# Rests of the first weight tiles by accumulating DMA instead of GpSimd, masks made one layer earlier, and another pool of banks for the last down steps (hybrid two-layer network, 1 core)

## The chip, the core and the metric

The kernel runs on one core of one Trainium2 chip. The metric is the device time of one execution in microseconds. A core has a matrix engine (PE), a vector engine (DVE), a scalar engine (ACT), GpSimd (POOL), a sync engine (SP) that issues most loads, and 16 DMA engines that all queues share.

## The reference

256 tokens of width 2048 go through two layers. Each layer is a mixer and a conv-FFN, and after each of the four comes a residual sum and a layer norm. All is in fp32.

```python
def conv_ffn(x, w_up, conv_w, conv_b, w_down):          # D_FF = 5632, CONV_W = 3
    h = x @ w_up
    hc = conv_b + conv_w[CONV_W - 1] * h
    for j in range(CONV_W - 1):
        hc = hc + conv_w[j] * shift_right(h, CONV_W - 1 - j)
    a, v = jnp.split(hc, 2, axis=-1)
    return (jax.nn.silu(a) * v) @ w_down
...
    for l in range(DEPTH):                               # DEPTH = 2
        if l % 2 == 0:
            mix = jnp.concatenate([ya, yb], axis=-1) @ ev_w_out[e]   # gated unit, window means
        else:
            h = x @ od_w_in[o]
            q, f_logit, inp, g = jnp.split(h, 4, axis=-1)
            y = hgrn2(q, f_logit, inp, lb_all[l])        # chunked linear recurrence, chunk mask tril
            y = rms_norm(y, ...) * jax.nn.sigmoid(g)
            mix = y @ od_w_out[o]
        x = layer_norm(ALPHA * x + mix, ln1_g[l], ln1_b[l])
        x = layer_norm(ALPHA * x + conv_ffn(x, ...), ln2_g[l], ln2_b[l])
```

## The kernel before, in words

**Split products.** PE multiplies numbers of type fp32r. A matrix `w` is therefore cut into a rounded part `wh` and a rest `wl = w - wh`, the activations likewise into `xh` and `xl`, and a product is summed from three matmuls, `xh*wh`, `xh*wl` and `xl*wh`. Weights come in raw tiles of 128 x 2048 fp32 (1 MB), three slots (`BUFS`), loaded by SP's queue in the order of a plan (`Weights`). `cast` (before L162 to L185) makes `wh` on ACT (L178) and `wl` by a subtraction (L181), into a ring of three pairs. A tile holds four blocks of 128 rows by 512 columns, so that one tile with one half of the tokens is 12 matmuls of 128x512. Tokens are in two halves, t = 0 and t = 1, and a stage's first `chunk` uses each of its four weight tiles first for one half, then for the other.

**Who subtracts.** `wl` is DVE's work, except for the first two tiles of each FFN and of the second layer's mixer: their numbers stand in the set `on_pool` (L168, filled in `plan_ffn` L227 and at L244), and GpSimd makes their rests, four pieces of 128x512 each.

**Heads of stages.** A stage ends with its last product, the residual sum into `x_t` (`add_x`, DVE L542 or L574), the statistics, and for each half t four pieces q = 0 to 3 of the normalization: DVE takes off the mean and multiplies by `g` (L511), multiplies by the inverse deviation `rs` and adds `b` (L512). PE then transposes a piece into `pt` (L493, four small matmuls), ACT writes `xh` from it (L279) and DVE `xl` (L280). The next stage's first product needs piece 0 of half 0. The work of a stage's end and of the next one's beginning is interleaved, and a scheduler puts each engine's instructions in one order ahead of time; an engine runs them strictly in that order. I call these three places head 1 (start of the first FFN, 240 us), head 2 (start of the second layer's mixer, 967 us) and head 3 (start of the second FFN, 1465 us).

**Banks.** PSUM has eight banks. Four are the pool `acc` (tags `ps0` to `ps3`) for the units of the FFN, which sum into them over many products; four are the pool `aux` for all else, transposes, `ph` and the down products `pd` among it. `down` (L563 on) multiplies one block of the gated hidden values by one tile of `w_down` for both halves into two `aux` banks, and DVE adds each to `x_t` (L574). The FFN's plan does four down steps beside each of the units 1 to 9, and two beside unit 10; the two left over come after unit 10 (L820 and L821), then `last_down` takes the last block.

**The masks.** The recurrence writes its attention products with a predicate `msk`, a byte tile of four copies of a triangular matrix `tri`. It is cast by DVE at the beginning of the second layer (L838 to L840).

Of the kernel before, what the change touches and what calls it, by code (L numbers as in the profile page):

```python
# [9 lines left out]
F32 = mybir.dt.float32  # L10
F32R = mybir.dt.float32r
BF16 = mybir.dt.bfloat16
U8 = mybir.dt.uint8
AF = mybir.ActivationFunctionType
ALU = mybir.AluOpType
# [3 lines left out]
P = 128  # L19
# [10 lines left out]
          ("P1", "s", "P7", "s", "P3", "P2", "P6", "o", "P5", "o", "P4", "s", "s"))  # L30
UNIT = ("P1", "s", "P2", "s", "P3", "o", "P7", "o", "P6", "o", "P5", "o", "P4", "s", "s")
BUFS = 3
EDGE = 244


class Weights:
# [3 lines left out]
    def __init__(self, nc, raw, hl, ahead):  # L40
        self.nc, self.raw, self.hl, self.ahead = nc, raw, hl, ahead

        self.feeds, self.loads = [], ([], [])
        self.n_load = [0, 0]

        self.phase = self.open = 0
        self.n_cast = self.n_take = self.n_prep = 0
        self.ring = {}
        self.done = {}
        self.on_pool = set()  # L50

        self.extra = {}

# [108 lines left out]
    def cast(self, pieces=1, between=None):  # L162
        i = self.n_cast
        w = self.feeds[i]["r"]["tile"]
        pool, tags = (self.raw[1], self.extra[i]) if i in self.extra else (self.hl, ("wh", "wl"))
        h = pool.tile([P, 4, 512], F32R, name=f"wh{i}", tag=tags[0])
        l = pool.tile([P, 4, 512], F32R, name=f"wl{i}", tag=tags[1])
        if i in self.on_pool:  # L168
            pieces, eng = 4, self.nc.gpsimd
        else:  # L170
            eng = self.nc.vector
        n = 4 // pieces
        self.prep(i + 1)
        for k in range(0, 4, n):
            if between is not None:
                between(k)
            sl = slice(k, k + n)
            self.nc.scalar.activation(h[:, sl], w[:, sl], AF.Copy)  # L178
            if k == 0:
                self.prep(i + 2)  # L180
            eng.tensor_tensor(out=l[:, sl], in0=w[:, sl], in1=h[:, sl].bitcast(F32), op=ALU.subtract)  # L181
        self.done[i] = (h, l)
        self.n_cast += 1
        if self.feeds[i]["after"]:
            self.feeds[i]["after"]()  # L185
# [17 lines left out]
def block_kernel(ctx: ExitStack, tc: tile.TileContext, a, out):  # L203
    nc = tc.nc
    V, A, G, T = nc.vector, nc.scalar, nc.gpsimd, nc.tensor

    const = ctx.enter_context(tc.tile_pool(name="const", bufs=1))
# [8 lines left out]
    acc = ctx.enter_context(tc.tile_pool(name="acc", bufs=1, space=PSUM))  # L216
    banks = ["ps0", "ps1", "ps2", "ps3"]
    aux = ctx.enter_context(tc.tile_pool(name="aux", bufs=4, space=PSUM))

    W = Weights(nc, raw, hl, 2)  # L220
# [3 lines left out]
        W.std([a["w_ev_out"][c, g] for g in (2, 3, 0, 1)])  # L224

    def plan_ffn(l):
        W.on_pool |= {len(W.feeds) + i for i in range(2)}  # L227
        W.extra[len(W.feeds) + 3] = ("q1", "q3")
        up, down = a["w_up"][l], a["w_down"][l]
        W.phase += 1  # L230
        for p in range(11):
            if p == 0:
                W.std([up[0, g] for g in range(4)])
                W.std([up[11, g] for g in range(4)])
                continue
            now = [down[c, p - 1] for c in range(4 if p < 10 else 2)]
            W.quad([up[p, 0], up[p, 1], up[11 + p, 1], up[11 + p, 0]],
                   [up[p, 2], up[p, 3], up[11 + p, 2], up[11 + p, 3]], now)
        W.std([down[c, 9] for c in (2, 3)])
        W.extra[len(W.feeds)] = ("q1", "q3")  # L240
        W.std([down[c, 10] for c in range(4)])

    plan_ffn(0)
    W.on_pool |= {len(W.feeds) + i for i in range(2)}  # L244
    W.extra[len(W.feeds) + 3] = ("qa", "qb")
    W.phase += 1
    wi, wo = a["w_od_in"], a["w_od_out"]
# [14 lines left out]

    edge.tile([P, EDGE], F32, name="edge")
    cst = const.tile([P, 3, P], F32, name="cst")
    ident, tri, aft = (cst[:, i] for i in range(3))
    mhalf = const.tile([P, 4], F32, name="mhalf")
    G.memset(mhalf, -0.5)


    def new_T(kind, g, pool=acts):  # L270
        h = pool.tile([P, 4, S], F32R, name=f"{kind}h{g}", tag=f"{kind}h{g}")
        l = pool.tile([P, 4, S], F32R, name=f"{kind}l{g}", tag=f"{kind}l{g}")
        return h, l
# [218 lines left out]
    def transpose(dst, src):  # L492
        T.transpose(dst, src, ident)  # L493
# [80 lines left out]
            V.tensor_tensor(out=xs, in0=xs, in1=ps, op=ALU.add)  # L574
        return xs

    def down(c, Ts, scale):

        w = W.take()
        for t in range(2):  # L580
            ps = aux.tile([P, 512], F32, name="pd", tag="aux")
            product(ps, w, Ts, t)
            tick(0.5)
            add_x(t, c, ps, scale)

    def last_down(get, g_ap, b_ap, final, n_skew=4):

        gt, bt = load_gb(g_ap, b_ap)
        sts = [small.tile([P, 4, 6], F32, name=f"st{t}") for t in range(2)]
        new = [new_T("x", g) for g in range(4)] if not final else None  # L590
        def out_bank():
            b = banks.pop(0)
            banks.append(b)
            return acc.tile([P, 512], F32, name="ps", tag=b)

        def after(t, c, ps):
            V.bn_stats(sts[t][:, c], add_x(t, c, ps, False))  # L597

        def norm(t, q, mean, rs):
            qs = slice(q * 512, (q + 1) * 512)  # L600
            normalize(x_t[t][:, qs], x_t[t][:, qs], mean, rs, gt[:, qs], bt[:, qs])
            if final:
                nc.sync.dma_start(out[t * P:(t + 1) * P, qs], x_t[t][:, qs])
            else:
                transpose_split(new[q], x_t[t][:, qs], t)

        tick(9)
        Ts = get()
        for c in range(4 - n_skew):
            w = W.take()  # L610
            for t in range(2):
                ps = out_bank()
                product(ps, w, Ts, t)
                after(t, c, ps)
        skewed = range(4 - n_skew, 4)
        ws = [W.take() for _ in skewed]
        for c, w in zip(skewed, ws):
            ps = out_bank()
            product(ps, w, Ts, 0)
            after(0, c, ps)  # L620
        mean, rs = moments(sts[0])
        todo = list(range(4))
        for c, w in zip(skewed, ws):
            ps = out_bank()
            product(ps, w, Ts, 1)

            while len(todo) > 3 - c:
                norm(0, todo.pop(0), mean, rs)
            after(1, c, ps)
        mean, rs = moments(sts[1])  # L630
        for q in range(4):
            norm(1, q, mean, rs)
        return new
# [4 lines left out]
    def lower_bound():  # L638
        lp = small.tile([P, 2, 16], F32, name="lp", bufs=1)
        nc.sync.dma_start(lp, a["lbT"].rearrange("p (l h) -> p l h", l=2))  # L640
        mx = small.tile([P, 16], F32, name="mx", bufs=1)
        V.tensor_tensor(out=mx, in0=lp[:, 0], in1=lp[:, 1], op=ALU.max)
        for l in range(2):
            V.tensor_tensor(out=lp[:, l], in0=lp[:, l], in1=mx, op=ALU.subtract)
        A.activation(lp, lp, AF.Exp)
        V.tensor_tensor(out=mx, in0=lp[:, 0], in1=lp[:, 1], op=ALU.add)
        V.reciprocal(mx, mx)
        for l in range(2):
            V.tensor_tensor(out=lp[:, l], in0=lp[:, l], in1=mx, op=ALU.mult)
        V.tensor_tensor(out=lp[:, 1], in0=lp[:, 0], in1=lp[:, 1], op=ALU.add)  # L650
        V.tensor_tensor(out=lp[:, 1], in0=lp[:, 1], in1=lp[:, 0], op=ALU.subtract)

        def store():
            pl = aux.tile([16, P], F32, name="pl", tag="aux")
            transpose(pl, lp[:, 1])
            row = small.tile([16, P], F32, name="row", bufs=1)
            A.activation(row, pl, AF.Copy)
            nc.sync.dma_start(lb_d, row)

        later(1, store)  # L660
# [5 lines left out]
    with tc.tile_pool(name="work0", bufs=1) as wk:  # L666
# [73 lines left out]
        gv, bv = loads0()  # L740
        chunk(XT, 4, after_v(1))
        lower_bound()
        for t in range(2):
            nc.sync.dma_start(x_t[t], a["x"][t * P:(t + 1) * P])
        chunk(XT, 4, after_b(0))
# [11 lines left out]
    def ffn(l, XT, final):  # L757
        with ExitStack() as pools:
            wk = pools.enter_context(tc.tile_pool(name=f"workf{l}", bufs=1))
# [8 lines left out]
            GT = {}  # L768
# [48 lines left out]
            for p in range(1, 11):  # L817
                downs = [lambda c=c, p=p: down(c, GT[p - 1], p == 1) for c in range(4)]
                strassen(XT, XS, h_tile, ready(p), downs[:4 if p < 10 else 2])
            for fn in downs[2:]:  # L820
                fn()  # L821
            XT = last_down(lambda: GT[10], a["ln2_g"][l], a["ln2_b"][l], final)
            del raw[1]
        return XT
# [4 lines left out]
    with ExitStack() as pools:  # L829
        yp = pools.enter_context(tc.tile_pool(name="ymix1", bufs=1))  # L830
        raw[1] = pools.enter_context(tc.tile_pool(name="rawq", bufs=1))
        wk = pools.enter_context(tc.tile_pool(name="work1", bufs=1))
# [2 lines left out]
        A.activation(tri_r, tri, AF.Copy)  # L835
        aft_r = wk.tile([P, P], F32R, name="aft_r")
        A.activation(aft_r, aft, AF.Copy)
        msk = wk.tile([P, 4, P], U8, name="msk")  # L838
        for k in range(4):
            V.tensor_copy(msk[:, k], tri)  # L840
        att = [wk.tile([P, 4, P], F32, name=f"att{t}") for t in range(2)]
        for t in range(2):
            G.memset(att[t], 0.0)
# [269 lines left out]
```

## Time and profile before

| what | value |
|---|---|
| median of 3 runs | 2197.44 us (2197.28 to 2199.90) |
| the profiled execution's own time | 2202.97 us |
| its span in the trace | 2201.2 us |
| busy: PE / weight loads / DVE / ACT / POOL | 2157.1 / 1779.9 / 1767.4 / 1230.3 / 125.8 us |
| moved by DMA | 489.00 MB |

The page gives busy time by engine, then 40 slices of the span, the DMA queues, the chain that ended last, and the costliest groups of instructions. Queries of the trace give more: `--timeline` lists an engine's instructions in order, with the idle time ahead of one and what ended it in brackets; the view of waits sums those brackets.

### The profile page before, as it was taken

What the parts mean: (1) busy time and instruction counts of PE and PEld (TensorE: products, weight loads), DVE (VectorE), ACT (ScalarE), POOL (GpSimd) and SP (SyncE); (2) the same over time, 40 slices, a digit from 0 to 9 for tenths busy, and PEclk for the clock granted to TensorE, in tenths of its full rate; (3) what the DMA queues carried; (4) which work ended last, traced back from release to release, by engine and by line L of the source; (5) the groups of instructions that cost most, each with busy time, mean ns of one, the idle gap of its engine ahead of it and who ended that gap; (6) DMA issues with size and microseconds to landing.
All of it is one profiled execution on the core that took longest, in us unless ns stands there. A gap on an engine that the chain in (4) does not pass through costs nothing. (4 is left out here: it accounts for less than half of the span.)

```text
span 2201.2 us, 24814 instructions
## 1 busy us (share of the span) xinstructions
PE 2157.1 (98%) x9887; PEld 1779.9 (81%) x9887; DVE 1767.4 (80%) x1706; ACT 1230.3 (56%) x1150; POOL 125.8 (6%) x140
## 2 busy tenths in 40 slices
PE   9999999999999999989999999999999999999997
PEld 7888788888888888878778888778888888888886
DVE  5545888888888888897687887888888888888888
ACT  5443455555655555646575756636555655555662
POOL 1000200000000000020000000030000000000000
PEclk9999999999999999999999999999999999999999
DMA  8646476777667677537778687746777666677743
GB/s 324 268 151 234 152 243 222 236 247 239 215 217 226 219 241 248 184 128 259 222 236 252 220 256 229 232 173 204 234 243 238 218 223 213 227 241 240 242 150 141
DMA packets 71796, 489.00 MB, mean 222 GB/s; under 512 B 8465, under 2 KB 9121, under 8 KB 13953
## 3 DMA queue, kind: packets, MB, share of 16 engines
q1 hardware_dynamic: 60656, 411.56, 50.0%
q0 software_dynamic: 11024, 75.86, 17.1%
q8 instruction: 77, 1.26, 0.2%
q14 instruction: 39, 0.31, 0.0%
HBM read 443.34 MB, written 2.11 MB: 202 GB/s over the span
## 5 line engine op out<-in xcount | busy, mean ns | idle before, releaser
L181 DVE TENSOR_TENSOR wl<-w,wh 128x2048 fp32r<-128x2048 f32 (+1 forms) x471 | 1051.2, 2235 | 337.7 <-ACT wh L178 334.2
L178 ACT ACTIVATE wh<-w 128x2048 fp32r<-128x2048 f32 (+1 forms) x495 | 894.7, 1813 | 628.7 <-PE pd L566 262.2
L412 PE MATMUL ps<-wh,xh 128*128 128x512 f32 x1188 | 468.0, 394 | 0.0
L412 PE MATMUL ps<-wl,xh 128*128 128x512 f32 x1188 | 462.8, 390 | 1.1 <-DVE wl L181 1.1
L412 PE MATMUL ps<-wh,xl 128*128 128x512 f32 x1188 | 462.8, 390 | 0.0
L566 PE MATMUL pd<-wh,yh 128*128 128x512 f32 x736 | 287.2, 390 | 3.2 <-DVE x L574 3.2
L566 PE MATMUL pd<-wl,yh 128*128 128x512 f32 x736 | 286.5, 389 | 0.4 <-DVE wl L181 0.4
L566 PE MATMUL pd<-wh,yl 128*128 128x512 f32 x736 | 286.4, 390 | 0.5 <-DVE yl L280 0.4
L412 PEld LDWEIGHTS ps<-wh,xl 128*128 128x128 f32 x1188 | 223.0, 188 | 46.7
L412 PEld LDWEIGHTS ps<-wl,xh 128*128 128x128 f32 x1188 | 223.3, 188 | 46.2 <-DVE wl L181 1.9
L412 PEld LDWEIGHTS ps<-wh,xh 128*128 128x128 f32 x1188 | 223.1, 188 | 45.0 <-ACT wh L178 0.4
L412 PE MATMUL ps<-wh,sh 128*128 128x512 f32 x432 | 169.8, 393 | 0.8 <-ACT u L424 0.5
L412 PE MATMUL ps<-wl,sh 128*128 128x512 f32 x432 | 168.9, 391 | 1.1 <-DVE wl L181 1.1
L412 PE MATMUL ps<-wh,sl 128*128 128x512 f32 x432 | 168.7, 390 | 0.0
L566 PEld LDWEIGHTS pd<-wh,yh 128*128 128x128 f32 x736 | 138.2, 188 | 32.5 <-DVE x L574 4.0
L566 PEld LDWEIGHTS pd<-wh,yl 128*128 128x128 f32 x736 | 138.1, 188 | 30.3 <-DVE yl L280 1.6
L566 PEld LDWEIGHTS pd<-wl,yh 128*128 128x128 f32 x736 | 138.2, 188 | 29.3 <-DVE wl L181 0.8
L341 PE MATMUL ps<-wh,xh 128*128 128x512 f32 x384 | 151.8, 397 | 1.6 <-ACT wh L178 1.6
L341 PE MATMUL ps<-wl,xh 128*128 128x512 f32 x384 | 151.2, 394 | 0.3 <-DVE wl L181 0.3
L341 PE MATMUL ps<-wh,xl 128*128 128x512 f32 x384 | 150.8, 393 | 0.0
L789 DVE SCALAR_TENSOR_TENSOR hc<-ph,cw,hc 128x254 f32<-128x254 f32 (+1 forms) x352 | 145.8, 475 | 1.4 <-ACT hc L786 1.2
L786 ACT ACTIVATE hc<-ph,cw 128x256 f32<-128x256 f32 x176 | 89.1, 556 | 62.5 <-DVE hc L789 58.8
(223 smaller groups left out, 2216.5 us busy)
## 6 DMA issues: line engine op xcount, KB each, us to landing
w<-in_w_up SPq DMA_DIRECT2D x176, 1024.0 KB, 4.9
w<-in_w_down SPq DMA_DIRECT2D x88, 1024.0 KB, 4.9
w<-in_w_od_in SPq DMA_DIRECT2D x64, 1024.0 KB, 6.6
w<-w POOLq DMA_DIRECT2D x40, 1024.0 KB, 8.1
w<-in_w_od_in POOLq DMA_DIRECT2D x21, 1024.0 KB, 9.2
w<-in_w_ev_in SPq DMA_DIRECT2D x20, 1024.0 KB, 5.2
w<-in_w_ev_out SPq DMA_DIRECT2D x16, 1024.0 KB, 4.8
w<-in_w_od_out SPq DMA_DIRECT2D x16, 1024.0 KB, 7.2
```

Source lines behind the costliest of these rows:

```text
L178: self.nc.scalar.activation(h[:, sl], w[:, sl], AF.Copy)
L181: eng.tensor_tensor(out=l[:, sl], in0=w[:, sl], in1=h[:, sl].bitcast(F32), op=ALU.subtract)
L341: T.matmul(ps[t], s[:, k, ts], m[:, k], start=(gi == 0 and k == 0 and i == 0), stop=(gi == n - 1 and k == 3 and i == 2))
L412: T.matmul(bank_, x[:, k, ts], m[:, k], start=(id(bank_) not in started), stop=(k == 3 and i == 2), skip_group_check=True)
L566: T.matmul(ps, x[:, k, t * P:(t + 1) * P], m[:, k], start=(k == 0 and i == 0), stop=(k == 3 and i == 2))
L786: A.activation(ob, pt[:, k], AF.Identity, scale=cw[:, 2, blk:blk + 1], bias=cw[:, 3, blk:blk + 1])
L789: V.scalar_tensor_tensor(out=ob[:, s:S], in0=pt[:, k, 0:S - s], scalar=cw[:, w, blk:blk + 1], in1=ob[:, s:S], op0=ALU.mult, op1=ALU.add)
```

## The change

1. **Rests.** `on_pool` becomes `on_dma`, with the same tiles. For each half (128x1024) of such a tile ACT writes `wh`, then ACT writes `wl = -wh`, and GpSimd's queue issues a DMA that adds the raw `w` into `wl` in memory (512 KB each). GpSimd computes nothing there, and ACT has four instructions of 128x1024 a tile where it had four of 128x512. The weights of the next tiles are prepared (`prep(i + 2)`) ahead of these.
2. **Masks.** `msk` becomes a constant tile; its four casts stand in the first layer, behind `lower_bound`. `EDGE` shrinks by the same 512 bytes a partition, so that the addresses behind it stay.
3. **Banks.** The two left-over down steps of each FFN (c = 2, 3) take banks of `acc` in turn (`out_bank`), which are the unit's, instead of `aux` banks.

```diff
-EDGE = 244
+EDGE = 244 - 128
...
-        if i in self.on_pool:
-            pieces, eng = 4, self.nc.gpsimd
-        else:
-            eng = self.nc.vector
+        if i in self.on_dma:
+            self.prep(i + 2)
+            for sl in (slice(0, 2), slice(2, 4)):
+                self.nc.scalar.activation(h[:, sl], w[:, sl], AF.Copy)
+                self.nc.scalar.activation(l[:, sl], h[:, sl].bitcast(F32), AF.Copy, scale=-1.0)
+                self.nc.gpsimd.dma_start(l[:, sl].rearrange("p k n -> p (k n)"),
+                                         w[:, sl].rearrange("p k n -> p (k n)"), accum_op=ALU.add)
+            self.done[i] = (h, l)
+            self.n_cast += 1
+            return
...
-            eng.tensor_tensor(out=l[:, sl], in0=w[:, sl], in1=h[:, sl].bitcast(F32), op=ALU.subtract)
+            self.nc.vector.tensor_tensor(out=l[:, sl], in0=w[:, sl], in1=h[:, sl].bitcast(F32), op=ALU.subtract)
...
+    msk = const.tile([P, 4, P], U8, name="msk")
...
-    def down(c, Ts, scale):
+    def out_bank():
+        b = banks.pop(0)
+        banks.append(b)
+        return acc.tile([P, 512], F32, name="ps", tag=b)
+
+    def down(c, Ts, scale, own=False):
...
-            ps = aux.tile([P, 512], F32, name="pd", tag="aux")
+            ps = out_bank() if own else aux.tile([P, 512], F32, name="pd", tag="aux")
...
         lower_bound()
+        for k in range(4):
+            V.tensor_copy(msk[:, k], tri)
...
-            for fn in downs[2:]:
-                fn()
+            for c in (2, 3):
+                down(c, GT[9], False, own=True)
...
-        msk = wk.tile([P, 4, P], U8, name="msk")
-        for k in range(4):
-            V.tensor_copy(msk[:, k], tri)
```

The order of the instructions moves at the heads. ACT at head 1 before: `w_40` and `w_41` are the first FFN's first two raw tiles, `xh` the four pieces of the new activations.

```order
L178 ACTIVATE wh_1589<-w_39_1497 128x2048
L178 ACTIVATE wh_1595<-w_40_1527 128x512 x4
L279 ACTIVATE xh_1157<-pt 128x4x128
L279 ACTIVATE xh_1159<-pt 128x4x128
L178 ACTIVATE wh_1607<-w_41_1563 128x512 x4
L279 ACTIVATE xh_1161<-pt 128x4x128
L279 ACTIVATE xh_1163<-pt 128x4x128
L178 ACTIVATE wh_1794<-w_42_1593 128x2048
```

ACT at head 1 in the change (its lines are numbered 7 or 8 higher):

```order
L185 ACTIVATE wh_1594<-w_39_1502 128x2048
L172 ACTIVATE wh_1600<-w_40_1532 128x1024 x2
L173 ACTIVATE wl_1601<-wh_1600 128x1024 x2
L172 ACTIVATE wh_1610<-w_41_1568 128x1024 x2
L173 ACTIVATE wl_1611<-wh_1610 128x1024 x2
L287 ACTIVATE xh_1162<-pt 128x4x128
L287 ACTIVATE xh_1164<-pt 128x4x128
L287 ACTIVATE xh_1166<-pt 128x4x128
L287 ACTIVATE xh_1168<-pt 128x4x128
L185 ACTIVATE wh_1795<-w_42_1598 128x2048
```

All eight casts of both tiles now stand ahead of the first `xh`; before, two pieces of `xh` stood between the tiles.

PE in head 1 before, at the first transposes of half 1 (`x_202`), which stood in the fourth tile (`wh_1800`):

```order
L341 MATMUL ps<-wh_1800,xh_1163 128x512
L493 MATMUL pt<-cst,x_202 128x128 x4
L341 MATMUL ps<-wl_1801,xh_1163 128x512
L493 MATMUL pt<-cst,x_202 128x128 x4
L341 MATMUL ps<-wh_1800,xl_1164 128x512
```

PE in head 1 of the change, where the same transposes (half 1 is `x_203` now) stand in the second tile (`wh_1610`):

```order
L349 MATMUL ps<-wh_1610,xh_1164 128x512
L349 MATMUL ps<-wl_1611,xh_1164 128x512
L501 MATMUL pt<-cst,x_203 128x128 x4
L349 MATMUL ps<-wh_1610,xl_1165 128x512
L501 MATMUL pt<-cst,x_203 128x128 x4
L349 MATMUL ps<-wh_1795,xh_1166 128x512
L349 MATMUL ps<-wh_1600,xh_1162 128x512
```

The transposes of half 1 moved up by some two tiles' products, and one more product of the third tile (`wh_1795`) stands behind them before half 1 begins with the first tile.

POOL at head 2, before (`w_132`, `w_133` are the mixer's first two tiles):

```order
L501 TENSOR_TENSOR rs<-rs,mhalf 128x1
L181 TENSOR_TENSOR wl_6695<-w_132_6638,wh_6694 128x512 x4
L181 TENSOR_TENSOR wl_6707<-w_133_6686,wh_6706 128x512 x4
L843 MEMSET att_6941 128x512
L843 MEMSET att_6942 128x512
L851 DMA lb<-lb_d 128x512
L501 TENSOR_TENSOR rs<-rs,mhalf 128x1
```

POOL at head 2 in the change:

```order
L509 TENSOR_TENSOR rs<-rs,mhalf 128x1
L174 DMA wl_6696<-w_132_6639 128x1024 x2
L851 MEMSET att_6933 128x512
L174 DMA wl_6706<-w_133_6687 128x1024 x2
L509 TENSOR_TENSOR rs<-rs,mhalf 128x1
L851 MEMSET att_6934 128x512
L859 DMA lb<-lb_d 128x512
```

The eight subtractions have become four DMA issues, and `rs` of half 1 stands behind those and one memset only.

## Rows read from the trace of the kernel before

**Rows 1.** The page's first part: busy time and share by engine.

```profile
PE 2157.1 (98%) x9887; PEld 1779.9 (81%) x9887; DVE 1767.4 (80%) x1706; ACT 1230.3 (56%) x1150; POOL 125.8 (6%) x140
```

**Rows 2.** PE's waits: engine, line, releaser, us in total, times, longest.

```profile
PE pt L493 <- DVE x L512: 10.8, 8, 2.7
```

**Rows 3.** Timeline of PE, head 1: start, us, instruction, [idle before <-releaser].

```profile
243.30 0.63 PE L493 MATMUL pt<-cst,x 128*128 128x128 f32 x4 [1.10 <-DVE x L512]
...
249.60 0.63 PE L493 MATMUL pt<-cst,x 128*128 128x128 f32 x4 [2.67 <-DVE x L512]
...
251.28 0.63 PE L493 MATMUL pt<-cst,x 128*128 128x128 f32 x4 [0.83 <-DVE x L512]
...
252.44 0.39 PE L341 MATMUL ps<-wh,yl 128*128 128x512 f32 x1
```

**Rows 4.** Timeline of DVE, head 1.

```profile
239.40 1.41 DVE L511 SCALAR_TENSOR_TENSOR x<-x,mv,g 128x512 f32<-128x512 f32 x2
...
243.07 3.47 DVE L511 SCALAR_TENSOR_TENSOR x<-x,mv,g 128x512 f32<-128x512 f32 x2
```

**Rows 5.** Timeline of POOL, head 1.

```profile
241.01 12.52 POOL L181 TENSOR_TENSOR wl<-w,wh 128x512 fp32r<-128x512 f32 x8 [0.44 <-ACT wh L178]
```

**Rows 6.** Timeline of ACT: a 128x1024 instruction early on, then head 1.

```profile
11.93 1.06 ACT L279 ACTIVATE xh<-xr 128x1024 fp32r<-128x1024 f32 x1 [0.62 <-DMA xr<-in_xT]
...
240.30 2.19 ACT L178 ACTIVATE wh<-w 128x512 fp32r<-128x512 f32 x4 [8.96 <-PE ps L341]
```

**Rows 7.** The DMA issues: transfer, queue, count, KB each, median us to landing.

```profile
w<-w POOLq DMA_DIRECT2D x40, 1024.0 KB, 8.1
...
lb<-lb_d POOLq DMA_DIRECT2D x4, 256.0 KB, 3.4
```

**Rows 8.** The DMA queues over the span: packets, MB, share of 16 engines.

```profile
q0 software_dynamic: 11024, 75.86, 17.1%
```

**Rows 9.** The DMA issues between 235 and 300 us.

```profile
w<-w POOLq DMA_DIRECT2D x1, 1024.0 KB, 12.3
```

**Rows 10.** Groups of POOL's instructions: count, busy us, mean ns, idle before.

```profile
L81 POOL DMA_DIRECT2D w<-w x20 | 17.2, 859 | 720.9 <-DMA w<-in_w_up 658.7 <-issue 62.2
```

**Rows 11.** Stretches: busy us of each engine, PEclk, DMA share, GB/s.

```profile
240.00:245.00 5.00, 3.90 (x22) 2.93 (x21) 5.00 (x6) 3.27 (x6) 4.56 (x4) 1.00 0.01 2
...
975.00:980.00 5.00, 3.09 (x15) 2.42 (x14) 4.29 (x8) 1.72 (x1) 3.07 (x5) 0.91 0.55 194
980.00:985.00 5.00, 5.00 (x23) 3.96 (x22) 3.39 (x6) 1.72 (x3) 0.00 (x0) 0.75 0.17 68
...
1465.00:1470.00 5.00, 3.49 (x13) 2.89 (x14) 5.00 (x7) 2.08 (x4) 5.00 (x4) 0.72 0.00 0
```

**Rows 12.** Timeline of PE, head 2.

```profile
967.68 0.66 PE L493 MATMUL pt<-cst,x 128*128 128x128 f32 x4 [0.99 <-DVE x L512]
...
972.32 0.66 PE L493 MATMUL pt<-cst,x 128*128 128x128 f32 x4 [1.24 <-DVE x L512]
...
979.02 1.03 PE L493 MATMUL pt<-cst,x 128*128 128x128 f32 x4 [1.91 <-DVE x L512]
```

**Rows 13.** Timeline of DVE, head 2.

```profile
974.93 2.08 DVE L840 CAST msk<-cst 128x128 uint8<-128x128 f32 x1
```

**Rows 14.** Timeline of PE, head 3.

```profile
1465.40 0.66 PE L493 MATMUL pt<-cst,x 128*128 128x128 f32 x4 [0.93 <-DVE x L512]
1467.17 1.05 PE L493 MATMUL pt<-cst,x 128*128 128x128 f32 x4 [1.11 <-DVE x L512]
```

**Rows 15.** Timeline of PE at the left-over down steps of both FFNs.

```profile
940.75 0.49 PE L566 MATMUL pd<-wh,yh 128*128 128x512 f32 x1 [1.66 <-DVE x L574]
...
2163.18 0.50 PE L566 MATMUL pd<-wh,yh 128*128 128x512 f32 x1 [1.54 <-DVE x L574]
```

**Rows 16.** Timeline of DVE at the end of the program.

```profile
2179.83 0.69 DVE L574 TENSOR_TENSOR x<-x,ps 128x512 f32<-128x512 f32 x1 [0.63 <-PE ps L566]
...
2196.50 1.41 DVE L512 SCALAR_TENSOR_TENSOR x<-x,rs,b 128x512 f32<-128x512 f32 x2
```

More of the change, by code (lines that the diff above doesn't have):

```diff
@@ L49, in __init__ @@
         self.done = {}
-        self.on_pool = set()
+        self.on_dma = set()
         self.extra = {}
@@ L226, in plan_ffn @@
     def plan_ffn(l):
-        W.on_pool |= {len(W.feeds) + i for i in range(2)}
+        W.on_dma |= {len(W.feeds) + i for i in range(2)}
         W.extra[len(W.feeds) + 3] = ("q1", "q3")
@@ L243, in block_kernel @@
     plan_ffn(0)
-    W.on_pool |= {len(W.feeds) + i for i in range(2)}
+    W.on_dma |= {len(W.feeds) + i for i in range(2)}
     W.extra[len(W.feeds) + 3] = ("qa", "qb")
@@ L590, in last_down @@
         new = [new_T("x", g) for g in range(4)] if not final else None
[L591 to L594, printed above, removed]
         def after(t, c, ps):
```

## The prediction

> **What bounds the kernel now.** I read the busy times first. PE is busy for 98% of the span [rows 1], so about 44 us are PE's idle time, and no change that leaves the matmuls alone can give more than a part of that. The view of PE's waits then says where to look: the largest item is transposes that wait for DVE's normalization, 10.8 us in eight waits [rows 2]. The timeline puts them at the heads of the stages: 1.10, 2.67 and 0.83 us in head 1, 4.60 in all [rows 3], 0.99, 1.24 and 1.91 in head 2, 4.14 in all [rows 12], 0.93 and 1.11 in head 3, 2.04 in all [rows 14]. DVE's and POOL's timelines say why DVE is late there. Two L511 ops took 1.41 us together just before GpSimd began its subtractions and 3.47 us beside them [rows 4, 5]: 0.70 against 1.74 us each, and a 128x128 cast of the mask was at 2.08 us [rows 13]. GpSimd's eight pieces last 12.52 us [rows 5], and so the slow stretch covers a whole head. The left-over down steps are a separate place: PE waits 1.66 and 1.54 us there for an `aux` bank that DVE has not yet added to `x_t` [rows 15].
>
> The execution that these rows come from took 2202.97 us, 5.5 over the median of the three runs, 2197.44. I make the sum as a difference to 2202.97 and take the same difference from the median. A difference under about 0.2%, 4.4 us, cannot be told from no change.
>
> **How soon a rest lands.** This is the price that before does not show: an accumulating DMA of 512 KB, alone on idle queues. The nearest row is the same kind of transfer at twice the size, 8.1 us from issue to landing [rows 7]. Its moving part can be bounded: queue 0's packets took 17.1% of 16 engines' 2201.2 us over 11024 packets [rows 8], 0.546 us each; a tile is 128 rows of 8 KB, 8 packets an engine, 4.4 us. Half the bytes take 2.2 less, hence 5.9 us, an estimate. From below the nearest row is 3.4 us for 256 KB that do not accumulate; from above 8.1 [rows 7], and 12.3 for the one tile that accumulated while loads ran [rows 9]. DMA stands almost still at the heads, 2 GB/s at 240 to 245 us [rows 11], so I take 5.9.
>
> The Trainium skill (DMA: Bandwidth & Descriptors, section on the anatomy of one DMA on the GpSimd path) fits a DMA as 2.0 us plus its bytes over 436 GB/s, 3.2 us for 512 KB. By that fit a 1 MB tile would land in 4.4 us where the row has 8.1 for accumulating ones, so the trace disagrees; by it the sum would be about -8 instead of -5.4.
>
> **Head 1.** Removed: 12.5 us of GpSimd's subtractions. DVE's ops go back to 0.70 us, the four pieces of half 0 are ready at about 241.4, 242.1, 244.3 and 245.0, and the three waits (4.60) go; the last matmul of the layer before, which ends near 252.6 [rows 3], ends near 247.8. Gain 4.8. Added: ACT has four instructions of 128x1024 a tile at 1.06 us, 4.24, where it had 2.19 [rows 6]. All eight stand ahead of the first `xh`: 240.3 + 8.5 = 248.8, and `xh` (0.6) at 249.4. PE therefore waits 1.6 us for `xh`, then 0.55 for `xl`, which DVE writes behind it. Tile 0's second half of `wl` costs about 0.4; tile 1's first half is written by 247.7, lands 5.9 later at 253.6, and costs about 0.9. Half 1's transposes stand some two tiles earlier than before, and DVE reaches their pieces about 1 us late. That is 4.45 of new waits, and a net gain of 0.3. With faster landings it would be 0.9, since ACT's chain stays; with 8.1 us a loss of 1.1.
>
> **FFN 0's end and head 2.** The bank wait of 1.66 [rows 15] goes, as the unit's four banks are empty by then; what is late next is DVE's `wl` of those down tiles, 0.35, so +1.3. The three waits of the head (4.14) go with GpSimd's slowing, and with them the dip of PE's clock: granted 0.91 and 0.75 of 2.4 GHz in the two stretches from 975 to 985 us, behind PE's emptiest stretch, cost (0.09 + 0.25) x 5 = 1.7 us [rows 11]. The masks, 2.08 us of DVE there in the longest row [rows 13], go too, which is part of the same gain; in the first layer the four casts lie in DVE's slack (0.2 us each where nothing slows them; without that cover 0.8 in all). Together 7.1. Against that PE waits 1.9 us for tile 0's rest, which lands near 971 (written at 965.1 by stepping through ACT's order, and 5.9 to land), and 1.4 in all for tile 1's halves and DVE's later pieces. Net 3.85; about 5 with a 4 us landing, 1.9 with 8.1. POOL's order matters here too: `rs` of half 1 stood behind eight subtractions, and now stands behind four DMA issues of 0.86 us [rows 10] and one memset. ACT also reloads its function table three times more in this stage; I cost that at nothing, since PE then works on products whose inputs are a tile ahead. Without that cover it is up to 3 us.
>
> **Head 3.** The waits of 2.04 go, and the dip of the clock to 0.72 in 1465 to 1470 [rows 11], some 1.4 us. New: `xh` again behind both tiles' casts, 1.6; `xl` behind it and tile 1's rest, together about 1.3. Net 0.5; 1.2 with short landings, a loss of 1.5 with 8.1.
>
> **The program's end.** The bank wait of 1.54 [rows 15] goes, but DVE sets the end from there (last op at 2196.50, with one idle piece of 0.63 behind PE [rows 16]). About half arrives: 0.8. Its bounds are 0 and 1.54.
>
> **Sum:** 0.3 + 3.85 + 0.5 + 0.8 = 5.4 us. Profile: 2202.97 - 5.4 = 2197.6; median: 2197.44 - 5.4 = **2192.0 us**. Each microsecond of landing is worth about 2.2 us over the three heads, so the change breaks even near 8.2 us of landing.
>
> **The rivals.**
> - *Landings of 8.1 us*, as of whole tiles [rows 7], because the latency and not the bytes makes them long. For it: the 256 KB row without accumulation needs 3.4, so little of the 8.1 may scale with size. The heads give -1.1, +1.9 and -1.5, the end 0.8: about 0, 2197.3. Chance 0.20.
> - *Short landings*, 4 us or under, on idle engines. For it: the 40 transfers behind 8.1 are spread over the FFNs' units, where weight loads run beside them, and here next to nothing moves [rows 11]. Heads 0.9 + 5.0 + 1.2, end 0.8: -7.9, 2189.5. Under 4 us ACT's chain binds and nothing more comes. Chance 0.22. The page's fit above speaks for it.
> - *Only the banks count*: the early transposes of half 1 wait as much as DVE's speed gives, so the heads give nothing beyond what the bank waits gave, 1.3 + 0.8: 2195.4. For it: new waits already eat 4.45 of 4.8 in head 1. Chance 0.08.
> - *Slower: rests come late.* A rest that lands as the one beside loads, 12.3 us [rows 9], holds PE, and with it the raw slots, whose loads and casts queue behind. It decides from 8.2 us of landing up; 4.2 us past 8.1 cost 2.1 each: +8.8, 2206. Against it: POOL issued its DMAs in 0.86 us [rows 10] while DVE was 80% busy, so a busy DVE does not hold an issue. Chance 0.10. The Trainium skill (SBUF — State Buffer, section on its two separate sides) says that GpSimd cannot write a DMA's descriptors while DVE runs an operation that takes the port they share, and DVE is never idle in these heads; by that the landings would be long. No row here shows such a stall.
>
> **How the numbers follow.** The forecast itself has 0.40, with a spread of its own from 2189.5 to 2195 for the terms that I put at nothing (the table loads) or at half (the end). Three quarters of it lie under 2193.0, the bound of faster by 0.2%: with the short landings 0.30 + 0.22, about 0.50 faster. Same: 0.10 + 0.20 + 0.08, about 0.40. Slower (over 2201.8): 0.10. The range of 8 in 10 runs from 2187.5, below the short landings, to 2199.0, above the landings of 8.1; it leaves out the late rests and the outer parts of the others.
>
> **What would show it.** Right: L511 and L512 at 0.70 us in all three heads; transposes of half 0 without a wait; PE waiting instead on ACT `xh` and on the DMA of `wl`, the halves landing in about 6 us; no `pd` wait at the ends of the FFNs; less of the clock's dip. Wrong: landings above 8 us, PE waits on `wl` above 2 us at a first tile, or table loads that PE waits for.

## The result and the profile after

The change is slower. Its median was 2211.04 us (7 runs, 2206.75 to 2219.52) beside 2202.91 us of the kernel before (7 runs): ratio 1.0051, 95% interval 1.0034 to 1.0068. A second comparison (e9 below) gave 2208.22 us (10 runs) beside 2201.58 (27 runs), ratio 1.0030 (1.0018 to 1.0042). So it costs some 7 to 11 us by the ratios; the forecast was 5.4 us faster. The median of three from which the forecast counted, 2197.44, lies 4 to 5 us below these medians of before, which touches its absolute time and not the difference.

The page's busy times, of after:

```profile
PE 2158.6 (98%) x9887; PEld 1778.0 (81%) x9887; DVE 1754.2 (80%) x1706; ACT 1243.8 (56%) x1153; POOL 98.8 (4%) x128
```

POOL lost 27 us of work and DVE 13 against [rows 1]; PE, which sets the time, gained nothing. PE's waits of after (engine, line, releaser, us, times, longest):

```profile
PE ps L349 <- DMA wl<-w: 11.5, 8, 3.6
...
PE pt L501 <- DVE x L520: 1.6, 2, 0.9
```

The second line answers to [rows 2]: 10.8 us of waits for the normalization became 1.6, as forecast, and no wait for a `pd` bank is left in the list. But 11.5 us of a wait that did not exist before stand on top. The timeline of PE in head 1 of after shows where:

```profile
248.78 0.50 PE L349 MATMUL ps<-wh,xh 128*128 128x512 f32 x1 [0.81 <-ACT xh L287]
...
250.07 0.50 PE L349 MATMUL ps<-wh,xl 128*128 128x512 f32 x1 [0.56 <-DVE xl L288]
...
253.28 0.50 PE L349 MATMUL ps<-wl,xh 128*128 128x512 f32 x1 [0.43 <-DMA wl<-w]
...
258.50 0.80 PE L349 MATMUL ps<-wl,xh 128*128 128x512 f32 x1 [3.56 <-DMA wl<-w]
```

The waits of [rows 3], 4.60 us, are gone, and 5.36 us of others came. DVE's row beside them, and ACT's:

```profile
242.08 1.41 DVE L519 SCALAR_TENSOR_TENSOR x<-x,mv,g 128x512 f32<-128x512 f32 x2
```

```profile
242.25 1.99 ACT L173 ACTIVATE wl<-wh 128x1024 fp32r<-128x1024 f32 x2
...
260.14 1.91 ACT L185 ACTIVATE wh<-w 128x2048 fp32r<-128x2048 f32 x1 [8.15 <-DMA w<-in_w_up]
```

DVE is at 0.70 us an operation where it had 1.74 [rows 4]. ACT's row at 260.14 is new: the cast of the fourth tile waited 8.15 us for its weights. The stretches of head 1 in after say why (busy us of each engine, PEclk, DMA share, GB/s):

```profile
240.00:245.00 5.00, 4.92 (x28) 3.79 (x27) 4.81 (x8) 4.56 (x5) 1.98 (x3) 1.00 0.00 2
245.00:250.00 5.00, 3.71 (x17) 2.48 (x16) 1.96 (x4) 5.00 (x8) 2.10 (x3) 1.00 1.07 210
250.00:255.00 5.00, 4.44 (x17) 3.04 (x17) 5.00 (x11) 1.99 (x2) 0.94 (x1) 1.00 1.05 190
255.00:260.00 5.00, 1.50 (x4) 1.21 (x5) 0.89 (x2) 0.00 (x0) 0.00 (x0) 0.70 0.80 251
260.00:265.00 5.00, 5.00 (x22) 4.18 (x21) 2.43 (x4) 2.99 (x3) 0.00 (x0) 0.61 0.47 192
```

From 245 to 255 us all 16 DMA engines are full (share 1.07 and 1.05) and move only 200 GB/s. In PE's emptiest stretch, 1.50 us of 5, its granted clock falls from 2.4 to 1.2 GHz: 0.70 is granted from 255 to 260 us and 0.61 in the next five. It fell while PE still stood idle, as this microsecond shows:

```profile
257.00:258.00 1.00, 0.00 (x0) 0.00 (x0) 0.00 (x0) 0.00 (x0) 0.00 (x0) 0.52 0.99 414
```

So of (0.30 + 0.39) x 5 = 3.45 us some 0.7 lie inside the wait of 3.56 that ends at 258.50, and about 2.7 us are lost on top of it; before, head 1 lost none. The balance of head 1: 5.36 + 2.7 - 4.60 = 3.5 us lost. The ledger below has 4.2; the rest lies in gaps too short for the timeline's brackets. The issues of the rests, with their landings over all twelve:

```profile
wl<-w POOLq DMA_DIRECT2D x12, 512.0 KB, 6.0
```

```profile
DMA to landing us min/median/max: 4.5/6.0/9.9
```

and SP's load into the first raw slot that comes free in head 1, of before and of after:

```profile
247.71 0.33 SPq L137 DMA_DIRECT2D w<-in_w_up  x1
```

```profile
250.70 0.33 SPq L137 DMA_DIRECT2D w<-in_w_up  x1
```

The slot is held 3 us longer, until the first tile's second half has landed. The load does not share the engines with the second tile's halves either, it stands behind them: the view of DMA queues from 245 to 255 us has packets of q0 alone, the queue that GpSimd issues to.

```profile
q0 software_dynamic: 536, 2.00, 106.0%
```

The load's first packet starts at 255.3 us, 4.6 after its issue (before: 0.95 after), and the load lands 9.35 us after its issue (before: 4.69). In head 1 no wait of PE follows from this. In head 2 one does: the load that was issued at 977.38 lands after 10.0 us, ACT's cast of the fourth tile waits for it, an `xh` of half 1 stands behind this cast on ACT, and on DVE the last piece of half 1's normalization stands behind the `xl` that needs this `xh`. PE waits for that piece, 0.88 us here and 2.78 us in the second profile.

```profile
987.41 1.92 ACT L185 ACTIVATE wh<-w 128x2048 fp32r<-128x2048 f32 x1 [4.79 <-DMA w<-in_w_od_in]
```

```profile
991.33 0.63 PE L501 MATMUL pt<-cst,x 128*128 128x128 f32 x4 [0.88 <-DVE x L520]
```

**A ledger by stages.** The two timelines of PE can be laid beside each other: the start of the same matmul (counted over those of 128x512) in each profile, and the change of that difference over a stage. Boundaries are the matmuls that start at 210, 299, 956, 1043, 1450 and 1541 us of before; every profile holds the same 8910 of these matmuls. Positive is longer than before, in us. The last column is PE's idle time in the three heads, summed from the timeline's brackets between the same boundaries; before has 10.8.

| kernel | head 1 | FFN 0 and its end | head 2 | rest of the mixer | head 3 | PE idle in the heads |
|---|---|---|---|---|---|---|
| change, first profile | 4.2 | -0.6 | 2.9 | -4.3 | 2.1 | 15.7 |
| change, second profile | 4.1 | -0.5 | 3.3 | 1.0 | 0.5 | 17.9 |
| e1 parts 2, 3 | 1.6 | -1.0 | 5.4 | -9.7 | 0.0 | 15.6 |
| e2 part 1 | 4.6 | -0.2 | 1.8 | -6.3 | 2.1 | 16.2 |
| e3 rests on DVE | -2.1 | -1.2 | -0.4 | -7.1 | 0.6 | 8.6 |
| e4 first tile by DMA | -2.4 | -0.7 | 0.0 | 3.9 | 1.8 | 9.8 |
| e5 writing DMAs | 2.2 | -1.3 | 0.3 | 2.2 | -0.9 | 11.5 |
| e6 first tile's adds only | 2.9 | -0.9 | 1.0 | -2.3 | -0.9 | 11.6 |
| e7 banks | 1.6 | -0.4 | -0.1 | 2.4 | -0.1 | 11.6 |
| e8 second tile by DMA | -1.2 | -1.0 | -2.2 | -6.9 | 0.7 | 8.7 |
| e10 second tile's second half | -4.1 | -0.9 | -1.5 | 2.1 | 3.3 | 9.4 |
| e11 as e8, without parts 2, 3 | -1.0 | 0.2 | -1.1 | -0.4 | 2.2 | 9.5 |
| e12 mixed | -4.0 | -1.1 | -1.9 | -1.4 | -0.1 | 5.8 |
| e13 writing, no negation | -1.5 | -0.8 | -5.9 | -4.2 | -1.0 | 5.0 |

The heads of the two profiles of one program agree within 0.4 us in heads 1 and 2 and within 1.6 in head 3. Part of every figure is PE's clock: a dip to 1.2 GHz that PE works through costs about 1.7 us, and it comes in one execution and not in another. The profile of before has a dip in heads 2 and 3 and none in head 1; e1 and e7, which have the same order on PE in head 1 and the same three waits there, have one in it, and 1.6 us stand in the table for that alone. So a difference under about 1.7 us says little about a head; the last column leaves the clock out. The rest of the mixer differs by 5.3 us between the change's profiles, -4.3 against 1.0: before has three dips there, the first profile one and the second two, and waits of 1 to 3 us fall differently. The first profile's 3.8 us over before (2205.0 against 2201.2) is thus flattered by 4.3 us that its heads did not earn.

### The profile page after: what moved, and what is told of

Read it like the earlier page. It is cut to its first block, busy times and chain, and to the rows that moved or that the text cites. A ratio compares the mean times of both kernels' runs of the same rounds, so it can differ in the third digit from the quotient of the medians.

```text
span 2205.0 us, 24813 instructions
## 1 busy us (share of the span) xinstructions
PE 2158.6 (98%) x9887; PEld 1778.0 (81%) x9887; DVE 1754.2 (80%) x1706; ACT 1243.8 (56%) x1153; POOL 98.8 (4%) x128
## 4 chain that ended last, share of the span: by engine, by line
PE 40%; DMA 4%; DVE 4%; ACT 2%; issue 2%; POOL 0%; DVEq 0%; POOLq 0%; ACTq 0%
PE ps L420 23%; PE pd L574 12%; DMA w<-in_w_od_in 2%; PE ps L349 2%; DVE wl L188 2%; PE ps L574 1%; ACT wh L185 1%; PE ph L501 1%; DMA w<-in_w_down 0%; POOL ss L509 0%; DMA wl<-w 0%; DMA lb<-lb_d 0%; DVE hc L799 0%; DVE o L992 0%; PE pa L951 0%
## 5 line engine op out<-in xcount | busy, mean ns | idle before, releaser
L185 ACT ACTIVATE wh<-w 128x2048 fp32r<-128x2048 f32 (+1 forms) x471 | 881.8, 1874 | 613.1 <-PE pd L574 254.4
L574 PE MATMUL pd<-wh,yl 128*128 128x512 f32 x704 | 273.9, 390 | 0.4 <-DVE yl L288 0.3
L574 PE MATMUL pd<-wh,yh 128*128 128x512 f32 x704 | 274.3, 390 | 0.0
L574 PE MATMUL pd<-wl,yh 128*128 128x512 f32 x704 | 274.0, 389 | 0.2 <-DVE wl L188 0.2
L349 PE MATMUL ps<-wl,xh 128*128 128x512 f32 x384 | 152.6, 399 | 11.8 <-DMA wl<-w 11.5
L574 PEld LDWEIGHTS pd<-wh,yl 128*128 128x128 f32 x704 | 132.1, 188 | 29.0 <-DVE yl L288 1.6
L574 PEld LDWEIGHTS pd<-wl,yh 128*128 128x128 f32 x704 | 132.2, 188 | 27.9 <-DVE wl L188 0.6
L574 PEld LDWEIGHTS pd<-wh,yh 128*128 128x128 f32 x704 | 132.1, 188 | 27.3
```

The source lines that it names most:

```text
L349: T.matmul(ps[t], s[:, k, ts], m[:, k], start=(gi == 0 and k == 0 and i == 0), stop=(gi == n - 1 and k == 3 and i == 2))
L574: T.matmul(ps, x[:, k, t * P:(t + 1) * P], m[:, k], start=(k == 0 and i == 0), stop=(k == 3 and i == 2))
```

## The experiments

Each was timed against the kernel before on the same chip: e1 to e4 on one chip, e5 to e8 on another, e9 to e13 on a third.

**Parts apart.** e1 keeps GpSimd's rests and has parts 2 and 3; its edit is the change's diff without the first part.

```diff
+        for k in range(4):
+            V.tensor_copy(msk[:, k], tri)
...
+            for c in (2, 3):
+                down(c, GT[9], False, own=True)
```

> Parts 2 and 3 of the change alone (masks in the first layer, banks of acc for the left-over down steps); the first tiles' rests stay with GpSimd. Theory A (the loss comes from the accumulating DMAs alone: four halves, 2 MB, run at about 200 GB/s, the last lands 9.9 us after its issue and the next weight load behind it): both waits of 1.66 and 1.54 us go, part comes back from DVE, so 1 to 3 us faster than before. Rival B (the other two parts cost, by a later DVE order at the ends of the FFNs): 2 us slower or more.

Measured: 2205.94 us beside 2201.06, ratio 1.0022 (1.0006 to 1.0038). Slower, as the rival had it, but not by its mechanism: the ends of the FFNs are not the place. The ledger puts the loss of its profile in head 2, 5.4 us. PE and DVE there:

```profile
987.40 0.87 PE L494 MATMUL pt<-cst,x 128*128 128x128 f32 x3 [6.49 <-DVE x L513]
```

```profile
984.78 0.43 DVE L858 TENSOR_SCALAR omlb<-lb 128x512 f32<-128x512 f32 x1 [5.73 <-DMA lb<-lb_d]
985.12 0.15 DVE L499 TENSOR_SCALAR rs<-mv 128x1 f32<-128x1 f32 x1
```

With four casts gone, the scheduler put `omlb` (one minus the bound `lb`) ahead of `rs` of half 1. `omlb` waits for a DMA that GpSimd's queue issues behind its eight subtractions, so half 1's normalization stood 5.73 us behind a transfer that it does not need. The change itself has the same masks but not this wait: there `omlb` stands behind the last piece of half 1's normalization on DVE (991.71 us). e7 is part 3 alone, with the casts back in their place:

```diff
-            for fn in downs[2:]:
-                fn()
+            for c in (2, 3):
+                down(c, GT[9], False, own=True)
```

> Part 3 alone (banks). In the run with parts 2 and 3 PE waited 6.49 us in head 2, because without the mask casts the order put omlb, which waits for the lb DMA behind GpSimd's work, ahead of the inverse deviation of half 1 on DVE. Theory F: with the casts back, omlb stands behind it again, that wait is gone, and the bank waits of 1.66 and 1.54 us too: 1 to 3 us faster than before. Rival B: the banks themselves cost, 3 us slower or more.

Measured: 2204.47 beside 2201.62, ratio 1.0009 (0.9992 to 1.0026): no difference that can be told, so the gain of 1 to 3 us is missed. The wait of 6.49 is gone (head 2 at -0.1), and so are the bank waits, but FFN 0's end gives only 0.4 of 1.66; at the program's end 1.1 of the 1.54 stay in this profile. The ratios of e1 and e7 overlap, so the price of the wait of 6.49 is read from the trace and not shown by a time.

e2 is part 1 alone:

```diff
-            pieces, eng = 4, self.nc.gpsimd
+            for sl in (slice(0, 2), slice(2, 4)):
+                self.nc.scalar.activation(h[:, sl], w[:, sl], AF.Copy)
+                self.nc.scalar.activation(l[:, sl], h[:, sl].bitcast(F32), AF.Copy, scale=-1.0)
+                self.nc.gpsimd.dma_start(l[:, sl].rearrange("p k n -> p (k n)"),
+                                         w[:, sl].rearrange("p k n -> p (k n)"), accum_op=ALU.add)
```

> Part 1 alone: rests by accumulating DMAs, masks and banks as before. Theory A: the whole loss and the gain of parts 2 and 3 on top, so 8 to 13 us slower than before, with waits on the DMA of wl as in the changed kernel. Rival B: no slower than 3 us.

Measured: 2206.25 beside 2201.06, ratio 1.0029 (1.0014 to 1.0045), 6 us. A little under the expected 8, and the interval begins at the rival's 3 us: the loss is the rests'. Head 1 is 4.6 us longer, as in the change.

**Is it the adding?** e5 lets the same twelve DMAs write instead of add.

```diff
-                                         w[:, sl].rearrange("p k n -> p (k n)"), accum_op=ALU.add)
+                                         w[:, sl].rearrange("p k n -> p (k n)").bitcast(F32R))
```

> The changed kernel with its twelve rest DMAs writing instead of adding (wl becomes w; the subtraction is left out), every engine's order the same. It prices the adding alone. Theory A (the adding DMAs run at about 200 GB/s and so queue behind each other and ahead of the next weight load): the rate doubles to some 400 GB/s, landings fall from 6.0 and 9.9 at most to about 3 to 4.5 us, PE's waits on them fall from 11.5 us to under 3, and the time falls by 6 to 10 us, to about before. Rival E (the adding costs no rate; issue and latency make the landings): landings within 0.5 us of 6.0, and the time as in the changed kernel, about 9 us slower than before.

Measured: 2200.28 beside 2201.62, ratio 0.9996 (0.9981 to 1.0011). That is 7 to 12 us under the change's ratios, as Theory A expected; PE's 9887 instructions stand in the change's order. The view of DMA issues, and the stretches of head 1:

```profile
wl<-w POOLq DMA_DIRECT2D x12, 512.0 KB, 3.4
```

```profile
245.00:250.00 5.00, 3.80 (x18) 2.56 (x16) 1.85 (x3) 5.00 (x8) 1.23 (x3) 1.00 0.84 263
250.00:255.00 5.00, 4.10 (x17) 3.04 (x17) 5.00 (x11) 2.35 (x3) 0.94 (x1) 1.00 0.99 337
```

The median landing falls from 6.0 to 3.4 us and the engines are full only at 337 GB/s. Two numbers missed: the longest landing is still 8.8 us, and PE's waits on these DMAs fall from 11.5 to 8.5 us, not under 3. The long ones are the last halves of a head, which now move beside the next load. The heads are 1.6 us longer than before in all, against 9.2 and 7.9 with the adding.

**Is it ACT's chain?** e6 keeps all of ACT's casts and leaves out the second tile's DMAs.

```diff
+                if i - 1 not in self.on_dma:
+                    self.nc.gpsimd.dma_start(l[:, sl].rearrange("p k n -> p (k n)"),
+                                             w[:, sl].rearrange("p k n -> p (k n)"), accum_op=ALU.add)
```

> The changed kernel without the second tile's two DMAs of each stage (its wl stays at -wh; that addition is left out). ACT's casts stay as they are, 8.0 us ahead of the first xh. Theory A: no landing over 6 us, no wait of 3.56 us in head 1, next weight load some 4 us earlier; 5 to 9 us faster than the changed kernel, so within 4 us of before. Rival D (ACT's chain ahead of the first xh sets the heads): still 6 us or more slower than before.

Measured: 2200.22 beside 2201.62, ratio 0.9984 (0.9966 to 1.0001). Rival D falls: with ACT's chain whole, the loss is gone. The landings are not as Theory A had them: the first tile's second half still takes 9.3, 8.8 and 8.8 us in the three heads, now beside the next load, which is issued 4.4 us earlier in head 1, and PE still waits 9.3 us for rests, in four waits of up to 3.65. PE's idle time in the heads falls by 4 to 6 us all the same. e13 takes ACT's second pass out of e5:

```diff
-                self.nc.scalar.activation(l[:, sl], h[:, sl].bitcast(F32), AF.Copy, scale=-1.0)
```

> The changed kernel with writing instead of adding DMAs and without ACT's second pass (wl = -h), which leaves the subtraction out altogether: ACT has 4 instead of 8 us of casts ahead of the first xh, and the DMAs start 2 us earlier. With the adding gone the three heads were still 2.5 us longer than before in their profile. Theory A': those are ACT's pass and the DMAs that start behind it; the heads become shorter than before by 4 us or more, and the time 4 to 8 us below before. Rival J (the transfers themselves, two 1 MB beside the loads): heads as with the pass, time within 2 us of before.

Measured: 2193.86 beside 2201.21, ratio 0.9956 (0.9937 to 0.9975), 9.7 us faster than before, a little more than expected; heads -1.5, -5.9 and -1.0, together 10.0 us below e5's (which are 1.6 longer than before by the table, not 2.5). So ACT's pass has a price too, once the adding is paid. Its instructions come in another order as well, so not all of the 10.0 is the pass itself.

**Which transfers hurt, and what to do instead.** e3 makes the rests in four pieces on DVE:

```diff
-            pieces, eng = 4, self.nc.gpsimd
+            pieces, eng = 4, self.nc.vector
```

> Parts 2 and 3, and the first two tiles' rests in four pieces on DVE: neither GpSimd nor a DMA makes them. Theory A: DVE's other operations run at 0.70 us and pay 8 x 0.69 = 5.5 us for the pieces, against about 8 us that GpSimd cost DVE in a head: 2 to 6 us faster than before. Rival C (DVE is the bound of the heads in any case, and 5.5 us more on it is 5.5 us more in each of three heads): 5 to 12 us slower than before.

Measured: 2200.65 beside 2201.06, ratio 0.9992 (0.9977 to 1.0007): neither. DVE is not the bound of the heads to the extent that Rival C needs, and the gain is too small to tell. e4 and e8 send one tile of the two by DMA and give the other to DVE as one operation; the edit is e4's, and e8 has `{len(W.feeds) + 1}` in its place:

```diff
-        W.on_dma |= {len(W.feeds) + i for i in range(2)}
+        W.on_dma |= {len(W.feeds)}
```

> The changed kernel, but only the first tile of each stage has its rests by DMA; the second tile's rest is one DVE operation (2.29 us). Theory A: 1 MB in two halves, landing in 4.5 to 6 us, none near 9.9, the raw slot free by 250 and the next load ahead by some 4 us in head 1: 1 to 6 us faster than before. Rival D (ACT's casts ahead of the first xh set the heads: 8.0 us of them now, 6 us here): still 3 to 5 us slower than before.

> The changed kernel with only the second tile's rests by DMA, the first tile's as one DVE operation (2.29 us). Theory A: 1 MB in two halves lands in 4.5 to 6 us, and nobody needs it before some 6 us of products of the first tile are done; 1 to 6 us faster than before. Rival G (the first tile's rest on DVE delays the normalization of half 0 by 2.3 us in each head): 2 to 5 us slower than before.

Measured: e4 2199.18 beside 2201.06, ratio 0.9994 (0.9980 to 1.0008); e8 2196.15 beside 2201.62, ratio 0.9986 (0.9970 to 1.0003). Neither can be told from before, so halving the adding transfers takes away the change's whole loss, whichever tile keeps them; the 1 to 6 us of gain that were expected are not shown. Landings were 4.5 to 6.1 us in e4 and 4.7 to 7.1 in e8. e10 sends only the second half (k = 2, 3) of the second tile by DMA, e11 is e8 without parts 2 and 3; e10's edit:

```diff
+            self.nc.scalar.activation(l[:, two], h[:, two].bitcast(F32), AF.Copy, scale=-1.0)
+            self.nc.gpsimd.dma_start(l[:, two].rearrange("p k n -> p (k n)"),
+                                     w[:, two].rearrange("p k n -> p (k n)"), accum_op=ALU.add)
...
+            self.nc.vector.tensor_tensor(out=l[:, one], in0=w[:, one], in1=h[:, one].bitcast(F32), op=ALU.subtract)
```

> Parts 2 and 3, the first tile's rest and the second tile's first half on DVE, only the second half of the second tile by one adding DMA of 512 KB a stage. Theory A: alone it lands in 4.5 to 5 us and PE waits on no such DMA; 3 to 8 us faster than before, and up to 3 faster than with both halves of the second tile by DMA. Rival G (DVE now makes 3/4 of the rests and is late for half 0): as before or slower.

> Only the second tile's rests by DMA, the first tile's on DVE, with the masks and banks of before. If parts 2 and 3 are worth 1 to 3 us with this, as theory F has it, this is 1 to 3 us slower than the run with them: 1 to 4 us faster than before. Rival B (parts 2 and 3 cost): faster than the run with them, 5 us or more faster than before.

Measured: e10 2199.98, ratio 0.9993 (0.9980 to 1.0005); e11 2198.23, ratio 0.9985 (0.9969 to 1.0001), both beside 2201.58: no difference that can be told, where e10 was expected 3 to 8 us faster. Its landings are 4.7 to 5.1 us as expected, and its head 1 is the shortest of all, -4.1; it gives that back in head 3, where PE waits 4.20 us for DVE's `wl` of the next tile. Parts 2 and 3 make no difference to e8 that can be told.

The change was timed again for a second profile:

> The change itself, unaltered, on the chip of the other runs, for a second profile of the same program. Theory A: 8 to 12 us slower than before, as the first time; the waits on the rests' DMAs at the same three places within 1 us each, while the waits inside the second layer's mixer and the dips of PE's clock move between executions. Rival H (the first comparison was one chip's): within 4 us of before.

Measured as above, 1.0030, 6.6 us: less than the 8 expected, and the interval begins at the rival's 4 us. The chip is that of e10 to e13 alone. The waits on the rests repeat (3.88 us in head 1, 11.4 in all).

e12 takes for each head the way that its own ledger priced lowest: half of the second tile in the first FFN, the second tile in the mixer, GpSimd as before in the second FFN.

```diff
+        W.on_dma.update({n + 1: "half"} if l == 0 else {n: "pool", n + 1: "pool"})
...
+    W.on_dma[len(W.feeds) + 1] = "whole"
```

> For each head the way that cost least in the profiles so far: first FFN, second half of the second tile by DMA and the rest on DVE (head 1 was 4.1 us shorter than before); mixer, both halves of the second tile by DMA, the first on DVE (2.3 shorter); second FFN, GpSimd as before (0). With the bank of the first FFN (0.6): the heads' prices add, so 5 to 8 us faster than before. Rival I (they do not add, since every version has another order of instructions and the waits inside the mixer move): within 3 us of before.

Measured: 2195.06 beside 2201.21, ratio 0.9970 (0.9956 to 0.9983), 6.1 us faster than before and, by the ratios, 13 to 18 us faster than the change. The prices do add: -4.0, -1.1, -1.9 and -0.1 for the three heads and FFN 0's end make -7.1. It beats both kernels.

## Why the prediction was wrong, step by step

- **What bounds the kernel, and what frees DVE** were right. DVE's operations fell from 1.74 to 0.70 us beside no GpSimd work, and the waits for half 0's normalization went.
- **How soon a rest lands** failed, and it is the step that turned the sign. Each half was priced as if it were alone on idle engines, because "DMA stands almost still at the heads". Four halves of one head follow within 6 us, and they fill all 16 engines at 200 GB/s: 2 MB need 10 us. The last one of each head landed after 9.9, 8.8 and 8.4 us, not 5.9. That the median is 6.0 beside the forecast 5.9 is luck: the price was for a half with nothing ahead of it, and the first half of each head landed in 4.5 us (e10's lone ones in 4.7 to 5.1); the median is one of halves that queue. The 8.1 us of a 1 MB adding transfer [rows 7] had the number in it, had the moving part (4.4 us a tile [rows 8]) been summed over the two tiles. The 4.4 is low itself: its mean of 0.546 us a packet takes in 1328 packets of 4 bytes, and the queue's packets of 8 KB took 0.66 us, 5.3 a tile.
- **The raw slots** were named in the last rival only. They are held until the halves have landed (250.70 instead of 247.71), the next load's packets start behind the other halves', and the fourth tile's cast waits 8.15 us for it in head 1 and 4.79 in head 2, where 0.88 and 2.78 us of PE's time follow.
- **Head 1**: forecast 0.3 gained, 4.2 and 4.1 lost. The wait for `xh` was 0.81, not 1.6, as ACT took 1.0 us for 128x1024. Tile 1's first half landed at 253.24, near the forecast 253.6, and cost 0.43 where 0.9 stood; tile 1's second half, for which the sum has no term, cost 3.56 (3.88 in the second profile). The clock fell at that idle stretch, which cost 2.7 us (1.7 in the second profile) and which the forecast had only as a gain elsewhere.
- **FFN 0's end and head 2**: forecast 3.85 gained, 2.3 and 2.8 lost. The bank wait did go, but only 0.5 to 0.6 of the 1.3 stayed. Four waits on the rests came, 0.81, 0.98, 0.89 and 1.79 us: tile 0's two are the forecast 1.9 nearly to the number, and tile 1's, with DVE's piece of 0.88 (2.78) behind the late load, are 3.56 (5.05) where 1.4 stood. The dip of the clock moved by 5 us in the first profile, to 980 to 990; the second has none in this head and lost as much.
- **Head 3**: forecast 0.5 gained, 2.1 and 0.5 lost. Both profiles have the waits on tile 1's rests, 0.95 and 2.09 us; what lies between them is a dip of the clock in the first and none in the second.
- **The program's end**: forecast 0.8, and this term held. PE's wait of 1.54 went, DVE's chain behind it took more than half of it back, and from the second FFN's last units to the end of the span the two profiles gained 0.5 and 0.7 us. The other runs with part 3 gained 0.6 to 1.1 there; e2 and e11, without it, lost 0.1 and gained 0.4.
- **The table loads** of ACT, put at nothing, stay open. Three more than before, 1.28 us each, come between 994 and 1031 us, and at 1034 PE waits 1.23 us (1.62) for ACT's `wh`, where before has no wait. e5 and e7 have the same loads and waits of 0.89 and 1.09; but e4, with no more loads than before, has one of 1.99. **The masks** were worth nothing by themselves, and in e1 their absence let the scheduler put a wait ahead of half 1.
- **The rival that came true** is the late rests, given 0.10 with 2206 us. Its price was about right by another working: not one long latency but a queue of the change's own making.
- The Trainium skill's fit (DMA: Bandwidth & Descriptors, section on the anatomy of one DMA on the GpSimd path) gives 3.2 us for 512 KB, an estimate; e5's writing DMAs landed in 2.9 at best and 3.4 in the median, so it agrees there, and adding ones needed 4.5 at best. The Trainium skill's rule on descriptors (SBUF — State Buffer, section on its two separate sides), that GpSimd cannot write them while DVE runs an operation that takes the port they share, is not what delayed the rests: the first half of head 1 was issued while DVE worked (busy 4.81 of 5 us there) and landed in 4.5 us, and POOL's issues took 0.84 to 0.93 us each, with DVE busy or idle. (That DVE is "never idle in these heads" was too strong as well: 4.29 of 5 us from 975 to 980 [rows 11].)

Not tried: a fourth raw slot, which would tell by a time what the held slot costs beside the full engines; the trace shows its path to PE in head 2 alone. Why a dip of the clock or a wait in the rest of the mixer comes in one execution and not in the next stays open.

## What to carry to other kernels

Price transfers that start together as one transfer on one resource: bytes over the rate that rows of the same kind show, not the landing of each; and count the buffer that they hold, since the next load starts behind it. Work taken off an engine should not be given to another all at once: all of it on DMA cost 7 to 11 us, half of it on DMA and half on the vector engine took that loss away (e4, e8), and a choice head by head was worth 6 us (e12). When a short idle stretch of PE appears, look at the granted clock behind it before believing the sum of the waits.

## What was unexpected of the hardware

- An adding DMA moves at about half the rate: all engines are full at 190 to 210 GB/s, and a 4 KB packet takes 328 ns in the median; writing, the same packets take 174 ns (e5), with 337 GB/s beside a load. Its issue on POOL takes longer too, 0.84 to 0.93 us against 0.53 to 0.58.
- A load on SP's queue that was issued while four adding halves were under way started its first packet 4.6 to 5.1 us after its issue in the three heads of the change; before, in the same places, 0.95 to 0.98 us.
- PE's clock dips to 1.2 GHz at five places in the profile of before (979, 1082, 1382, 1443 and 1467 us), 1.7 us lost at each; the second profile of the change has three such places, 259, 1089 and 1389 us. One program's executions spread over 7 to 17 us, and over all runs the mean granted clock goes from 0.991 to 0.998.
